# Modulation sums moved ahead, one block sum made by an accumulating DMA, FFN parts 8-6-8, other V banks, and queues ordered by the scheduler's other time line

## The chip, the cores and the metric

The kernel runs on one core of a Trainium2 chip. The metric is the device time of one execution in microseconds, the median over several runs. Before the change it is 997.38 us (three runs, 997.08 to 998.87).

## The reference

One decoder layer on 512 tokens of width 1024, batch 1, everything in float32: a half-step SwiGLU FFN (d_ff 2816), a token mixer, and a second half-step FFN. Each of the three is pre-RMSNorm with shift, scale and gate computed from a conditioning vector c:

```python
mod = silu(c) @ w_mod + b_mod
sh1, sc1, ga1, sh2, sc2, ga2, sh3, sc3, ga3 = split(mod, 9)
h = modulate(rms_norm(x, g_ffn1), sh1, sc1)
x = x + 0.5 * (1 + ga1) * ((silu(h @ w1_gate) * (h @ w1_up)) @ w1_down)
h = modulate(rms_norm(x, g_mix), sh2, sc2)
x = x + (1 + ga2) * hybrid_mixer(h, w_in, b_f, g_q, g_k, w_o)
h = modulate(rms_norm(x, g_ffn2), sh3, sc3)
x = x + 0.5 * (1 + ga3) * ((silu(h @ w2_gate) * (h @ w2_up)) @ w2_down)
```

The mixer projects h to q, k, v of 8 stick-breaking heads and 8 forgetting-attention heads of width 64 and to 8 forget gates, runs causal attention of both kinds, and projects the joined heads back.

## The kernel before, in words

**Numbers.** A float32 operand is split into `hi`, a copy rounded to the fast matmul type (ACT casts it), and `lo`, the rest (DVE subtracts). A product is three matmuls, hi by hi, hi by lo, lo by hi (`mm3`, L129 to L132). Tokens lie along the free axis: x and h are 8 tiles of 128 x 512 each, and h exists as `h["h"]` and `h["l"]`.

**Weights.** A weight tile of 128 x 1024 comes by a DMA on SP's queue into a `raw` buffer (4 of them), then ACT casts `hi` and DVE makes `lo` (4 buffers each). The chain raw, hi, lo runs some products ahead of TensorE as far as the buffers allow. ACT, DVE, POOL and SP each work off their queue in order, so an instruction that waits holds all that stand behind it.

**The FFN** (`ffn`, L508). The 22 tiles of d_ff are done in three parts, `FPARTS` (L21), of 8, 8 and 6. A part computes its gated tiles, `a[j]` as `ah` and `al` (`gated`, L406: ACT's Silu into `sg`, DVE's product `av`, ACT's cast `ah`, DVE's `al`), and then its down projection (`down`, L578): for each of the 8 output chunks e one weight tile, as many tiles by 3 matmuls as the part has (512 columns each), `update` of x[e] by DVE (L574). In most parts tiles come in pairs, `block_pair` (L442): the gate and up products of two tiles are done with a 2 x 2 block scheme that needs 7 products of 24 matmuls of 256 columns instead of 8. It loads four weight blocks r11, r12, r21, r22 into the four raw buffers and forms on DVE (`combined`, L459, into `bsum` buffers) s1 = r21 + r22, s2 = s1 - r11, s3 = r11 - r21, s4 = r12 - s2. The order of the products is r11, s2, s1, r12, s3, s4, r22. In the first FFN tiles 0 to 7 are done singly and 8 to 21 in 7 pairs; in the second tiles 4 to 21 in 9 pairs.

**The modulation.** mod has 9 x 8 chunks of 128 numbers. Two of the nine are needed at once; the other 56 chunks are filled into the first FFN (`mod_next`, L232): each is one 512 KB load on SP's queue into a `wm` buffer (4, shared with the `bsum` tiles) and one DVE multiply with a running sum (L216, `junk`). Before: 2 after each of tiles 4 to 7, 2 after each output chunk of a down projection (L598), 1 after each block pair (L529); of the 56, 47 are called for by the end of the last pair.

**The turn** (`turn`, L642). At the end of the first FFN and of the mixer, the last three output chunks are done in two halves of the tokens (H0, H1), each in a pass of as many steps as the part has tiles (mixer: 8). While the second pass runs, the norm of the first half is made: `mean` is asked for ahead of step 5 of that pass, ACT and DVE make the reciprocal root, and `make` the new h. The second half's norm follows inside the next stage, after its first matmuls (`finish`).

**The first V products** (L745 to L754). The mixer starts with two weight chunks by four token blocks, in two groups `sp` of four products each. A product takes one PSUM bank. Eight banks exist under four tags: mm 3, z 2, pt 2, o 1. Both groups take mm, z, mm, z. `v_out` copies a finished bank into V on DVE or ACT.

**What sets the order.** Each instruction is traced in program order; the framework's scheduler simulates the engines and lays out each engine's queue, earlier program order first among what is ready. Inside `manual_schedule` the program order itself is kept: for all engines in the first stage, for TensorE alone in the turns, the first V products and the mixer.

Of the kernel before, what the change touches and what calls it, by code (L numbers as in the profile page):

```python
# [12 lines left out]
ALU = mybir.AluOpType  # L13
# [4 lines left out]
D = 1024  # L18
KD = D // P
NF = 22  # L20
FPARTS = (8, 8, 6)  # L21
SPLIT1 = tuple(range(8, NF, 2))
SPLIT2 = tuple(range(4, NF, 2))
NPAIR = 4
# [11 lines left out]
def hybrid_layer(  # L36
# [18 lines left out]
    nc = tc.nc  # L55
# [176 lines left out]
    def mod_next(n):  # L232
        for _ in range(min(n, len(mod_queue))):
            m, d = mod_queue.pop(0)
            mod_chunk(m, d)
            if d < KD - 1:
                continue
            nc.vector.tensor_tensor(mod_col(m), mod_col(m), cols[:, m * KD : (m + 1) * KD], op=ALU.add)
            if m in (2, 8):
                nc.vector.tensor_scalar(g_col(m), mod_col(m), 1.0, 0.5, op0=ALU.add, op1=ALU.mult)  # L240
            elif m == 5:
                nc.vector.tensor_scalar(g_col(m), mod_col(m), 1.0, 1.0, op0=ALU.add, op1=ALU.mult)
            elif m == 4:
                g_norm(m, C_GM, 0, KD)
            elif m == 7:
                g_norm(m, C_G2, 0, KD)
# [193 lines left out]
        return out  # L440

    def block_pair(w, n_w, j, T, tmp):  # L442
        raws = []
        for n in range(4):
            raw = wpool.tile([P, 2 * S], F32, tag="raw", name=nm("raw"), bufs=4)
            nc.sync.dma_start(raw, w[n_w + n])
            raws.append(raw)
        r11, r12, r21, r22 = raws

        def parts(src):  # L450
            hi = wpool.tile([P, 2 * S], F32R, tag="hi", name=nm("hi"), bufs=4)
            lo = wpool.tile([P, 2 * S], F32R, tag="lo", name=nm("lo"), bufs=4)
            nc.scalar.copy(hi, src)  # L453
            nc.vector.tensor_tensor(lo, src, hi.bitcast(F32), op=ALU.subtract)  # L454
            return hi, lo

        def combined(x0, x1, op):
            t = block_tile(tmp)
            nc.vector.tensor_tensor(t, x0, x1, op=op)  # L459
            return t  # L460

        def whole_h(k0, sl):
            return [(h["h"][k0 + k][:, sl], h["l"][k0 + k][:, sl]) for k in range(KD // 2)]

        def summed_h(n):
            sl = slice(n * 256, (n + 1) * 256)
            return [(hi[:, sl], lo[:, sl]) for hi, lo in T]

        def product(b, wt, rhs, first, last):
            for u, sl in enumerate((H0, H1)):  # L470
                for k, (rh, rl) in enumerate(rhs):
                    lh, ll = wk(wt, 4 * u + k)
                    f, e = first and u == 0 and k == 0, last and k == KD // 2 - 1
                    nc.tensor.matmul(b[:, sl], lh, rh, start=f, stop=False, skip_group_check=True)  # L474
                    nc.tensor.matmul(b[:, sl], lh, rl, start=False, stop=False, skip_group_check=True)  # L475
                    nc.tensor.matmul(b[:, sl], ll, rh, start=False, stop=e, skip_group_check=True)  # L476

        def result(x0, x1, out=None):
            if out is None:
                out = tmp.tile([P, S], F32, tag="bres", name=nm("bres"), bufs=4)  # L480
            nc.vector.tensor_tensor(out, x0, x1, op=ALU.add)
            return out

        bx, by, bz = bank("o"), bank("mm"), bank("z")
        product(bx, parts(r11), whole_h(0, H0), True, True)
        p1 = tmp.tile([P, S], F32, tag="bres", name=nm("bres"), bufs=4)
        nc.scalar.copy(p1, bx)
        s1 = combined(r21, r22, ALU.add)
        s2 = combined(s1, r11, ALU.subtract)
        product(by, parts(s2), summed_h(1), True, True)  # L490
        q = result(by, p1)
        product(bz, parts(s1), summed_h(0), True, True)
        r = result(bz, p1)
        product(bx, parts(r12), whole_h(4, H0), False, True)
        s3 = combined(r11, r21, ALU.subtract)
        product(by, parts(s3), summed_h(2), False, True)
        c22 = result(by, r, r)
        s4 = combined(r12, s2, ALU.subtract)
        product(bz, parts(s4), whole_h(4, H1), False, True)
        c12 = result(bz, q, q)  # L500
        product(by, parts(r22), summed_h(3), False, True)
        c21 = result(by, p1, p1)
        return [
            gated(j, [(H0, bx[:, H0], bx[:, H1]), (H1, c12[:, H0], c12[:, H1])], tmp),
            gated(j + 1, [(H1, c22[:, H0], c22[:, H1]), (H0, c21[:, H0], c21[:, H1])], tmp),
        ]

    def ffn(first, w, wd, gm, startup, boundary, tmp, finish=None, split=()):  # L508
        pend = list(kb) if startup else []
        blocks = {}  # L510
        n_w = 0
        f0 = 0
        for part, nf in enumerate(FPARTS):
            last_part = part == len(FPARTS) - 1
            a = []
            halves_first = first and part == 0
            units = {}
            j = -1
            while j + 1 < nf:
                j += 1  # L520
                f = f0 + j
                if f in split:
                    if "T" not in blocks:
                        blocks["T"] = block_sums(tmp)
                    a += block_pair(w, n_w, j, blocks["T"], tmp)
                    n_w += 4
                    j += 1
                    if startup:
                        mod_next(1)  # L529
                    continue  # L530
                ps = []
                for u in range(2):
                    if pend:
                        ps.append(pend.pop(0))
                        continue
                    if halves_first and j < 2:
                        if j == 0 and u == 0:
                            ws, bs = [], []
                            for i in range(4):
                                ws.append(prep(w[n_w], D, nc.gpsimd if i == 3 else None))  # L540
                                n_w += 1
                                bs.append(bank("mm" if i % 2 == 0 else "z"))
                            late = [(i, k) for i in range(4) for k in range(KD // 2, KD)]
                            for sl in (H0, H1):
                                early = [(i, k) for k in range(KD // 2) for i in range(4)]
                                for i, k in early + (late if sl is H1 else sorted(late, key=lambda s: s[1])):
                                    lh, ll = wk(ws[i], k)
                                    mm3(bs[i][:, sl], lh, ll, h["h"][k][:, sl], h["l"][k][:, sl], k == 0, k == KD - 1)
                                    if sl is H0 and (i, k) == (3, 0):
                                        finish()  # L550
                            in_order.__exit__(None, None, None)
                            units = dict(enumerate(bs))
                        ps.append(units[2 * j + u])
                        continue
                    wt = prep(w[n_w], D)
                    n_w += 1
                    b = bank("z" if u else "mm")
                    for k in range(KD):
                        lh, ll = wk(wt, k)
                        mm3(b, lh, ll, h["h"][k], h["l"][k], k == 0, k == KD - 1)  # L560
                    ps.append(b)
                a.append(gated(j, [(FULL, ps[0], ps[1])], tmp))
                if startup and f > 3:
                    mod_next(2 if part == 0 else 3)
            if startup and part == 0:
                blocks["T"] = block_sums(tmp)
            if last_part and boundary != "end":
                in_order.__enter__()
            done = down(wd, a, f0, nf, gm, boundary if last_part else None, tmp)
            f0 += nf  # L570
        return done
# [172 lines left out]

    chunks = [v_weights(2), v_weights(3)]  # L745
    for sp in range(2):
        grp = [(ch, s, bank("mm" if s % 2 == 0 else "z")) for ch in chunks for s in (2 * sp, 2 * sp + 1)]
        for k in range(KD):
            for ch, s, b in grp:
                v_step(ch, s, k, b)  # L750
            if sp == 0 and k == 0:
                finish()
        for ch, s, b in grp:
            v_out(ch[0], s, b)  # L754
# [483 lines left out]
```

## Time and profile before

| | before |
|---|---|
| median of 3 runs | 997.38 us |
| the profiled execution, device time | 999.74 us |
| its span, first to last instruction | 998.0 us |
| mean granted TensorE clock | 0.993 |
| DVE, ACT, POOL busy | 773.7, 439.0, 119.0 us |
| HBM read | 125.92 MB |

The stages, in us from the span's start: norm and first weights to 23; the first eight products with modulation to 61; the rest of part 0 to 104.7 and its down projection to 148.2; four pairs to 229.0 and the down projection of part 1 to 273.6; three pairs to 334.0 and the down projection of part 2, with the turn, to 374.4; the mixer, with its turn, to 645; the second FFN to 994. A row of the table by stage has the stretch, its length, then for PE (matmul), PEld (weight load), DVE, ACT and POOL the busy time and in brackets the number of instructions that touch the stretch, then the granted TensorE clock (1.00 is full speed), the mean share of the 16 DMA engines, and GB/s. In a timeline or a list of groups, `out<-in` names tiles; a number in square brackets is idle time of the engine before the instruction, and what ended it. A row of waits names the waiting engine, tile and line, then who it waited for, and us in total, times, and the longest.

### The profile page before, as it was taken

To read this page: it belongs to the slowest core of one execution; us is meant where nothing else is said; L and a number is where in the kernel's file an instruction comes from. 1 tells how busy PE (TensorE), PEld (TensorE's weight loads), DVE (VectorE), ACT (ScalarE), POOL (GpSimd) and SP (SyncE) were. 2 spreads that over 40 slices of the span, in tenths; PEclk is the share of its full clock that TensorE was granted. 3 is DMA by queue.
4 is the path that set the end of the run, shared out by engine and by line. 5 is a ranking of instruction groups with operands and counts; after the bars stand their busy time and mean duration, and the time that the engine had idled before them with its cause. 6 is when DMAs were issued, how large, how long until landed. Compare 5 with 4: busy or idle time off the path is not lost.

```text
span 998.0 us, 15752 instructions
## 1 busy us (share of the span) xinstructions
PE 976.3 (98%) x6284; PEld 869.4 (87%) x6284; DVE 773.7 (78%) x1147; ACT 439.0 (44%) x686; POOL 119.0 (12%) x131
## 2 busy tenths in 40 slices
PE   8999999999999898999999999999999999999998
PEld 7888889998899798877887877998988999889997
DVE  7999967999879966688857687698855699556962
ACT  6344224443244425587556462364432444324430
POOL 1000000000000043065413335210000000000000
PEclk9999999999999899999999999999999999999999
DMA  9985933359634832411212111214252133521231
GB/s 358 316 277 154 343 135 106 121 159 309 235 104 122 260 107 65 127 55 53 64 54 73 44 43 65 85 37 133 76 147 93 55 116 103 150 85 64 96 117 63
DMA packets 37369, 129.04 MB, mean 129 GB/s; under 512 B 4400, under 2 KB 4656, under 8 KB 37296
## 3 DMA queue, kind: packets, MB, share of 16 engines
q1 hardware_dynamic: 35712, 125.88, 38.1%
q10 hardware_dynamic: 1584, 2.16, 0.6%
q8 instruction: 49, 0.80, 0.3%
q14 instruction: 24, 0.20, 0.1%
HBM read 125.92 MB, written 2.10 MB: 128 GB/s over the span
## 4 chain that ended last, share of the span: by engine, by line
PE 76%; DVE 14%; ACT 4%; DMA 3%; issue 2%; POOL 1%; SPq 0%; ACTq 0%; DVEq 0%; POOLq 0%
PE pt L131 8%; PE pt L132 8%; PE pt L130 8%; PE mm L130 5%; PE mm L132 4%; PE mm L131 4%; PE mm L476 3%; PE mm L475 3%; PE mm L474 3%; PE o L476 3%; PE o L475 3%; PE o L474 2%; PE z L476 2%; PE z L475 2%; PE z L474 2%; DVE lo L454 2%
## 5 line engine op out<-in xcount | busy, mean ns | idle before, releaser
L125 ACT CAST hi<-raw 128x1024 fp32r<-128x1024 f32 (+2 forms) x90 | 91.5, 1021 | 142.3 <-PE pt L131 61.3
L131 PE MATMUL pt<-al,hi 128*128 128x512 f32 (+1 forms) x334 | 131.1, 392 | 2.5 <-DVE al L415 2.5
L130 PE MATMUL pt<-ah,hi 128*128 128x512 f32 (+1 forms) x334 | 130.4, 391 | 0.6 <-ACT ah L414 0.6
L132 PE MATMUL pt<-ah,lo 128*128 128x512 f32 (+1 forms) x334 | 130.4, 390 | 0.0
L126 DVE TENSOR_TENSOR lo<-raw,hi 128x1024 fp32r<-128x1024 f32 (+2 forms) x89 | 108.0, 1216 | 28.8 <-ACT hi L125 28.3
L453 ACT CAST hi<-bsum 128x1024 fp32r<-128x1024 f32 x64 | 66.8, 1051 | 113.5 <-DVE bsum L459 61.3
L474 PE MATMUL mm<-th,hi 128*128 128x256 f32 x384 | 108.7, 283 | 0.0
L475 PE MATMUL mm<-tl,hi 128*128 128x256 f32 x384 | 108.7, 283 | 0.0
L476 PE MATMUL mm<-th,lo 128*128 128x256 f32 x384 | 108.7, 283 | 0.0
L574 DVE SCALAR_TENSOR_TENSOR x<-pt,gcol,x 128x512 f32<-128x512 f32 (+1 forms) x51 | 36.3, 712 | 67.2 <-PE pt L132 67.2
L454 DVE TENSOR_TENSOR lo<-bsum,hi 128x1024 fp32r<-128x1024 f32 x64 | 78.2, 1222 | 10.8 <-ACT hi L453 10.3
L453 ACT CAST hi<-raw 128x1024 fp32r<-128x1024 f32 x48 | 50.4, 1050 | 67.5 <-PE pt L131 30.5
L130 PE MATMUL mm<-hh,hi 128*128 128x512 f32 (+1 forms) x208 | 79.6, 383 | 0.0
L132 PE MATMUL mm<-hh,lo 128*128 128x512 f32 (+1 forms) x208 | 77.9, 374 | 0.6 <-DVE lo L126 0.6
L131 PEld LDWEIGHTS pt<-al,hi 128*128 128x128 f32 x334 | 63.4, 190 | 16.8 <-DVE al L415 4.0
L131 PE MATMUL mm<-hl,hi 128*128 128x512 f32 (+1 forms) x208 | 77.8, 374 | 0.2 <-DVE hl L170 0.2
L130 PEld LDWEIGHTS pt<-ah,hi 128*128 128x128 f32 x334 | 63.3, 190 | 14.4 <-ACT ah L414 1.4
L132 PEld LDWEIGHTS pt<-ah,lo 128*128 128x128 f32 x334 | 63.4, 190 | 12.9
L474 PEld LDWEIGHTS mm<-th,hi 128*128 128x128 f32 x384 | 73.7, 192 | 0.0
L475 PEld LDWEIGHTS mm<-tl,hi 128*128 128x128 f32 x384 | 73.7, 192 | 0.0
L476 PEld LDWEIGHTS mm<-th,lo 128*128 128x128 f32 x384 | 73.7, 192 | 0.0
L476 PE MATMUL o<-hh,lo 128*128 128x256 f32 x256 | 72.4, 283 | 0.0
(349 smaller groups left out, 2565.6 us busy)
## 6 DMA issues: line engine op xcount, KB each, us to landing
raw<-w SPq DMA_DIRECT2D x80, 512.0 KB, 3.6
wm<-wmod SPq DMA_DIRECT2D x72, 512.0 KB, 5.2
raw<-w1d SPq DMA_DIRECT2D x16, 512.0 KB, 6.3
raw<-wqk SPq DMA_DIRECT2D x16, 512.0 KB, 3.5
raw<-w2d SPq DMA_DIRECT2D x16, 512.0 KB, 4.2
raw<-w1s SPq DMA_DIRECT2D x8, 512.0 KB, 5.3
raw<-wo SPq DMA_DIRECT2D x8, 512.0 KB, 3.5
raw<-w1d SPq DMA_DIRECT2D x8, 384.0 KB, 5.9
```

The costliest lines, as they stand in the source:

```text
L125: nc.scalar.copy(hi, raw)
L126: (lo_engine or nc.vector).tensor_tensor(lo, raw, hi.bitcast(F32), op=ALU.subtract)
L130: nc.tensor.matmul(ps, lh, rh, start=first, stop=False)
L131: nc.tensor.matmul(ps, lh, rl, start=False, stop=False)
L132: nc.tensor.matmul(ps, ll, rh, start=False, stop=last)
L453: nc.scalar.copy(hi, src)
L454: nc.vector.tensor_tensor(lo, src, hi.bitcast(F32), op=ALU.subtract)
L474: nc.tensor.matmul(b[:, sl], lh, rh, start=f, stop=False, skip_group_check=True)
L475: nc.tensor.matmul(b[:, sl], lh, rl, start=False, stop=False, skip_group_check=True)
L476: nc.tensor.matmul(b[:, sl], ll, rh, start=False, stop=e, skip_group_check=True)
L574: nc.vector.scalar_tensor_tensor(out=x[e][:, sl], in0=ps[:, sl], scalar=g_col(gm)[:, e : e + 1], in1=x[e][:, sl], op0=ALU.mult, op1=ALU.add)
```

## The change

Six edits. (1) The parts of both FFNs are 8, 6, 8. (2) In `block_pair` s1 is no longer added by DVE: d21 is loaded into a raw buffer and d22 is added onto it by a second DMA that accumulates, issued from POOL's queue; the raw buffers then hold s1, r11, r12, r22. (3) s3 is formed as r22 - s2, which is the same r11 - r21. (4) Modulation: 3 chunks after each pair but the last, where there are none; the single tiles stay at 2. (5) The second group of the first V products takes banks pt, mm, pt, o. (6) The scheduler works against its other simulated time line (`schedule_with_timeline_sim`), which can change the order of every queue that isn't kept by hand.

```diff
-FPARTS = (8, 8, 6)
+FPARTS = (8, 6, 8)
...
     def block_pair(w, n_w, j, T, tmp):
-        raws = []
-        for n in range(4):
+        d11, d12, d21, d22 = (w[n_w + n] for n in range(4))
+
+        def load(src):
             raw = wpool.tile([P, 2 * S], F32, tag="raw", name=nm("raw"), bufs=4)
-            nc.sync.dma_start(raw, w[n_w + n])
-            raws.append(raw)
-        r11, r12, r21, r22 = raws
+            nc.sync.dma_start(raw, src)
+            return raw
+
+        s1 = load(d21)
+        nc.gpsimd.dma_start(s1, d22, accum_op=ALU.add)
+        r11, r12, r22 = load(d11), load(d12), load(d22)
...
-        s1 = combined(r21, r22, ALU.add)
         s2 = combined(s1, r11, ALU.subtract)
...
-        s3 = combined(r11, r21, ALU.subtract)
+        s3 = combined(r22, s2, ALU.subtract)
...
                     if startup:
-                        mod_next(1)
+                        mod_next(3 if f < NF - 2 else 0)
...
                 if startup and f > 3:
-                    mod_next(2 if part == 0 else 3)
+                    mod_next(2)
...
     for sp in range(2):
-        grp = [(ch, s, bank("mm" if s % 2 == 0 else "z")) for ch in chunks for s in (2 * sp, 2 * sp + 1)]
+        tags = iter(("pt", "mm", "pt", "o") if sp else ("mm", "z", "mm", "z"))
+        grp = [(ch, s, bank(next(tags))) for ch in chunks for s in (2 * sp, 2 * sp + 1)]
...
-    with tile.TileContext(nc) as tc:
+    with tile.TileContext(nc, schedule_with_timeline_sim=True) as tc:
```

## The prediction

> **What bounds the kernel now.** First the page: TensorE is busy for 976.3 of 998.0 us, so what isn't matmul time is 22 us at most, and the question is where it lies and whether the change reaches it.
>
> ```profile
> span 998.0 us, 15752 instructions
> PE 976.3 (98%) x6284; PEld 869.4 (87%) x6284; DVE 773.7 (78%) x1147; ACT 439.0 (44%) x686; POOL 119.0 (12%) x131
> ```
>
> Second, the view of waits, TensorE's alone: who it waited for, us in total, times, longest.
>
> ```profile
> PE mm L724 <- ACT hh L167: 2.8, 1, 2.8
> PE pt L131 <- DVE al L415: 2.5, 3, 1.1
> PE z L724 <- ACT V L713: 0.9, 1, 0.9
> PE pt L130 <- ACT ah L414: 0.6, 1, 0.6
> PE mm L131 <- DVE hl L170: 0.2, 1, 0.2
> ```
>
> Third, the table by stage, cut where TensorE's output tile changes (length, then busy us of PE, PEld, DVE, ACT, POOL, granted clock, DMA share, GB/s).
>
> ```profile
> 104.70:148.24 43.54, 43.54 (x193) 36.04 (x192) 35.00 (x50) 9.07 (x9) 0.00 (x0) 1.00 0.63 233
> 168.40:188.56 20.16, 20.16 (x171) 20.16 (x170) 19.32 (x26) 9.79 (x14) 0.00 (x0) 1.00 0.42 132
> 148.24:228.96 80.72, 80.72 (x674) 80.69 (x673) 71.79 (x89) 37.98 (x52) 0.00 (x0) 1.00 0.42 136
> 228.96:273.55 44.59, 44.00 (x194) 35.96 (x193) 39.20 (x58) 10.95 (x12) 0.00 (x0) 1.00 0.76 274
> 273.55:334.02 60.47, 60.47 (x505) 60.47 (x504) 53.83 (x70) 27.20 (x38) 0.00 (x0) 1.00 0.44 134
> 334.02:360.58 26.56, 23.99 (x92) 18.72 (x91) 20.65 (x31) 8.14 (x11) 10.66 (x7) 0.87 0.63 211
> 336.00:340.90 4.90, 2.39 (x9) 1.10 (x7) 4.90 (x10) 3.30 (x5) 0.00 (x0) 0.90 1.00 312
> 340.90:347.80 6.90, 6.84 (x18) 5.41 (x19) 6.73 (x10) 2.49 (x3) 1.61 (x1) 0.57 0.75 267
> 377.38:380.93 3.55, 3.55 (x14) 3.21 (x15) 3.55 (x10) 2.06 (x5) 0.00 (x0) 0.52 0.43 147
> 412.00:460.00 48.00, 43.95 (x218) 33.49 (x217) 39.73 (x66) 36.67 (x71) 24.20 (x26) 0.99 0.22 67
> 460.00:632.00 172.00, 169.09 (x1154) 138.61 (x1153) 122.28 (x198) 89.54 (x182) 63.85 (x68) 0.99 0.16 53
> 669.91:961.13 291.22, 290.59 (x1995) 271.46 (x1993) 212.97 (x249) 117.47 (x155) 0.00 (x0) 1.00 0.33 103
> 961.13:990.03 28.90, 28.90 (x129) 23.53 (x127) 11.25 (x15) 5.30 (x8) 0.00 (x0) 1.00 0.23 82
> ```
>
> These rows give TensorE's own pace. A down projection of 8 chunks by 8 tiles is 192 matmuls of 512 columns in 43.54 us: 0.2268 each. A block pair is 7 products of 24 matmuls, 168 of 256 columns in 20.16 us: 0.120 each. Held against it, the second FFN (669.91 to 961.13) loses nothing that could be won, and the loss sits in three places. (1) In the first FFN where block pairs give way to a down projection: 44.59 for 43.54 at 228.96, 1.05 lost; and at 334.02 26.56 us for 90 matmuls of 512 columns (5 chunks, 6 tiles, 3), which at full pace take 20.4: 6.1 lost, of it some 3 in waiting and 2.8 in the stretch behind, 18 matmuls in 6.9 us at a clock of 0.57. (2) At the turn to the mixer: the wait of 2.8 for the first h tile, then 3.55 us at a clock of 0.52 (1.7 lost), then 0.9 for a PSUM bank. (3) The mixer: 4.05 and 2.91 us not busy, many small waits.
>
> Why 334.02 is so bad shows in the timeline of ACT and DVE there:
>
> ```profile
> 333.99 0.83 ACT L125 CAST hi<-raw 128x768 fp32r<-128x768 f32 x1 [3.58 <-DMA raw<-w1d]
> 336.68 1.28 ACT L98 ACT_TABLE_LOAD   x1
> 336.12 1.22 DVE L216 SCALAR_TENSOR_TENSOR junk<-wm,c_bc 128x1024 f32<-128x1024 f32 x1
> 337.27 0.69 DVE L415 TENSOR_TENSOR al<-av,ah 128x512 fp32r<-128x512 f32 x1
> ```
>
> ACT stands 3.58 us on a cast of a down weight that lands late, with the last Silu queued behind it; DVE puts a modulation sum (L216) ahead of the al that TensorE waits for. Both are the modulation's doing: its loads stand before the down weights in SP's queue, its sums fill DVE.
>
> **The change part by part.** Sums go against the profiled execution, 999.74 us (998.0 span, 1.7 around it); the median of the runs is 997.38, 2.4 lower, and I take the same difference off that.
>
> *Parts 8, 6, 8.* The number of matmuls stays. Over the last part of each FFN the chunks that are cut into halves (3 at the first, 1 at the end) get 2 more tiles each: (3+1) x 2 x 3 = 24 matmuls of 512 columns become 48 of 256, 24 x (0.240 - 0.2268) = +0.3 us. In exchange each pass of the turn has 8 steps for 6. The mean of the first half is asked for at step 5 of the second pass; from there 13 steps of 3 x 0.12 are left now, 4.7 us, and 19 afterwards, 6.8: 2.1 us more cover over the wait of 2.8. The trace holds the same function with 8 steps per pass at the mixer's end, where the wait is 0.2 (L131 on hl). I take that: -2.6. The half clock that follows only this turn goes with it: -1.7.
>
> The last pairs-to-down transition now has 8 tiles, so the last al is due at the 22nd matmul, 4.8 us in, not at the 16th. It has no modulation left (next item) and resembles those of the second FFN, which lose nothing. The table load of 1.28 is still there; I leave 0.5 for it: -6.1 + 0.5.
>
> The middle transition gets 6 tiles, with modulation around it. Today with 8 tiles it loses 1.05; the last al is now due two tiles, 6 x 0.2268 = 1.4 us, earlier: 2.4 us lost, +1.4. Bounds: 0.3, the row 961.13 (28.90 for 126 matmuls, 28.58 at full pace: 6 tiles without modulation), and 6.1, the row 334.02 (6 tiles with it, and with a half clock behind). It is nearer to 1.05, since the table load isn't there: I take 2.4.
>
> *Modulation: 3 sums per pair instead of 1, none at the last.* The 56 sums stay; by the code 9 of them come behind the last pair today and none afterwards. From 148.24 to 334 DVE has 25:
>
> ```profile
> L216 DVE SCALAR_TENSOR_TENSOR junk<-wm,c_bc 128x1024 f32<-128x1024 f32 x25 | 30.5, 1220 | 2.9 <-DMA wm<-wmod 2.8
> L459 DVE TENSOR_TENSOR bsum<-raw,raw 128x1024 f32<-128x1024 f32 x12 | 14.7, 1222 | 3.5 <-DMA raw<-w 3.3
> raw<-w SPq DMA_DIRECT2D x80, 512.0 KB, 3.6
> wm<-wmod SPq DMA_DIRECT2D x72, 512.0 KB, 5.2
> raw<-w1d SPq DMA_DIRECT2D x8, 384.0 KB, 5.9
> GB/s 358 316 277 154 343 135 106 121 159 309 235 104 122 260 107 65 127 55 53 64 54 73 44 43 65 85 37 133 76 147 93 55 116 103 150 85 64 96 117 63
> ```
>
> Afterwards up to 9 more fall there, 9 x 1.3 = +12 us of DVE; the additions of s1 go, 7 x 1.2 = -8.5. From 148.24 to 334.02 DVE is busy 71.79 + 39.20 + 53.83 = 164.8 of 185.8 us, 89%; afterwards some 168 less 2 (shorter down weights) of 175 (the middle down is 48 x 0.2268 = 10.9 us shorter), 95%. On average it fits. The middle down is where it doesn't: per chunk TensorE needs 18 x 0.2268 = 4.1 us, in which two modulation tiles and one weight tile, 1.44 MB, want 353 GB/s; the best slice has 358, the stretch with all queues full 312. At 312 the 8 chunks' 11.5 MB take 36.9 us for 32.7: 4 us behind, covered by what SP loads ahead, or not. Bounds 0 and +4; nearer to the covered side, since at 274 GB/s the DMAs are at a share of 0.76: +1. What is queued behind: on SP the next down weight, for which ACT's cast, then all of ACT, waits.
>
> *s1 added by the DMA.* One DVE addition per pair goes, 16 in all. In the second FFN nothing waits for it, so nothing is won there; in the first its gain is in the 95% above. New is an accumulating load on POOL's queue that waits for d21. Behind it on POOL nothing stands in pair stages (POOL 0.00 in all their rows). With it and two more modulation tiles a pair loads 1.6 MB more, 132 GB/s becoming some 210, which collides with nothing. How long the accumulate takes, no row shows. Its room is read from one pair, which starts at 208.72:
>
> ```profile
> 204.77 1.22 DVE L459 TENSOR_TENSOR bsum<-raw,raw 128x1024 f32<-128x1024 f32 x1 [0.92 <-DMA raw<-w]
> 206.24 1.22 DVE L459 TENSOR_TENSOR bsum<-bsum,raw 128x1024 f32<-128x1024 f32 x1
> 212.12 1.22 DVE L454 TENSOR_TENSOR lo<-bsum,hi 128x1024 fp32r<-128x1024 f32 x1
> ```
>
> s1's last reader (lo, 212.12) ends 4.6 us into the pair, then the buffer may be loaded for the next; s2 is formed 2.5 us before the next pair (206.24 before 208.72). 20.16 - 4.6 - 2.5 = 13 us, less 3.6 for the plain load: 9.4 us for the accumulate. The nearest rows: 3.6 for a plain load, and 11.8 for twice the 5.9 of one under load, since it reads two sources. I take some 6 to 7, hidden: 0.
>
> The Trainium skill, "DMA: Bandwidth & Descriptors", section on SWDGE, HWDGE and iDMA, says that accumulation is only for transfers whose descriptors GpSimd writes into SBUF rings, and its section on the anatomy of one DMA fits them with 2.0 us plus the bytes by 436 GB/s, an estimate of 3.2 us here, which would leave the sum as it is. "GPSIMD Engine Reference", Key points, speaks against the change: GpSimd contends for SBUF with DVE instructions of two SBUF inputs, which are most of what DVE does in a pair. No run here shows either yet.
>
> *Other banks for the first V products.* The second group takes pt, the third mm, pt and o, all idle since the turn; the wait for the evacuation of a z bank goes: -0.9. Next late is nothing: the scores' first banks come later.
>
> *Other time line.* It reorders queues, not work. In the second FFN, with DVE at 213 of 291 us, there is room for any sane order. In the mixer the order decides; bounded by its own idle time, -7, and by all its 220 us waiting like the worst stretch, 4.05 of 48: 18.6, less the 7 that are there, +11.6. Nothing in the trace favours a side: 0.
>
> Sum: +0.3 - 2.6 - 1.7 - 5.6 + 1.4 + 1 - 0.9 = -8.1 us, 989.3.
>
> **The rivals.** *The loss moves to the middle transition and stays as large.* For it: the same tile count and the same modulation flood as at 334.02 today, more of it per pair. Against: no table load, and 1.05 today. Then 6.1 instead of 2.4 and 4 instead of 1: -8.1 + 3.7 + 3 = -1.4, 996.0, no change.
>
> *The mixer's queues get worse.* For it: nothing else in the change touches it, and its norm chains cross four engines. Against: today's order has no claim to be good. Priced above: -8.1 + 11.6 = +3.5, 1000.9, slower. It decides against the change from some 10 us of new waits in 412 to 632.
>
> *The accumulate lands too late* in every pair: each us over 9.4 costs 16. At 11.8 it is +38 - 8 = +30, 1027; the change is lost from 9.9 on.
>
> *The half clock isn't owed to these waits.* At 334 the longest is 1.1 us and they sum to some 3; then 2.8 and 1.7 stay lost: -8.1 + 4.5 = -3.6, 993.8, still faster. The Trainium skill, "TensorE: Matmul & The Clock Gate", section on HAM oscillation, has the clock halved by idle gaps over some 3.4 us; by that rule no wait here (1.1 and 2.8 at most) would do it. The trace disagrees so far: both halvings follow right behind waits.
>
> **How the numbers follow.** Forecast 989.3 (the likeliest case's own range 983 to 995.3): 0.59. Half clock stays: 0.05. Loss moved: 0.13. Mixer worse: 0.15. Accumulate late: 0.08. A measurement of this kernel can tell about 0.2%, 2 us. Faster 0.64, same 0.13, slower 0.23. The low end is the sum with the residues (0.5, 1.4, 1) gone and 3 of the mixer's 7 won: 983. The high end takes in the mixer's case with some us beyond: 1003; the accumulate's case and tails are left out.
>
> **What would show it.** Right: the wait L724 on hh at 0.2 or so and no clock under 0.9 between 300 and 400 us; no L216 after the last pair; the last down at 0.2268 per matmul; the wait of L724 on V gone; the middle down some 35 us long. Wrong: a middle down of 38 us or more with waits on al or ah and a half clock behind (loss moved); waits at s2's casts in every pair of both FFNs (accumulate); the mixer longer by several us.

## The result, and the profile after

The change makes the kernel slower: 1029.02 us median (4 runs, 1026.73 to 1031.45) beside 998.12 for the kernel before, run beside it, ratio 1.0321 with a 95% interval of 1.0301 to 1.0342. The forecast was 989.3 with a range up to 1003.0. The profiled execution took 1026.73 us, its span is 1025.0, the mean granted clock 0.987 (0.993 before).

From the page of the kernel after, the span, the engines' busy times, and two rows of POOL's accumulating load (the group of its issues, then the row of issues with the median time to landing):

```profile
span 1025.0 us, 15857 instructions
PE 985.1 (96%) x6308; PEld 874.9 (85%) x6308; DVE 753.2 (73%) x1131; ACT 440.6 (43%) x686; POOL 130.2 (13%) x147
L451 POOL DMA_DIRECT2D raw<-w x16 | 14.0, 878 | 520.5 <-DMA raw<-w 165.9
raw<-w POOLq DMA_DIRECT2D x16, 512.0 KB, 5.5
```

DVE has 20 us less to do, as the dropped additions say, and yet TensorE's time without matmul grows from 22 to 40 us. Its busy time grows by 8.8 us with 24 matmuls more, which at full clock would be 0.3: the rest is matmuls at a lower clock. So what was lost is waits and what follows waits. For the table by stage the runs are cut at the same places of the program. The last down reaches to the second step of the first V products (behind the matmul of the second half's mean); what is called the mixer reaches from there to the second pass of its turn; what is called its turn is that pass and the four single tiles of the second FFN; what is called the second FFN starts with its first block pair. After first (three pairs, the middle down, four pairs, last down, mixer, its turn, second FFN), then before (mixer, its turn, second FFN):

```profile
147.74:208.82 61.08, 60.68 (x505) 60.51 (x504) 55.37 (x76) 28.73 (x39) 0.86 (x1) 1.00 0.63 205
208.82:249.91 41.09, 35.70 (x146) 27.86 (x145) 36.34 (x58) 8.92 (x12) 1.72 (x2) 0.96 0.85 263
249.91:332.76 82.85, 80.85 (x673) 80.67 (x672) 71.62 (x93) 39.56 (x53) 1.72 (x2) 1.00 0.51 160
332.76:384.59 51.83, 50.02 (x286) 43.65 (x285) 24.89 (x39) 17.59 (x27) 11.25 (x9) 0.97 0.30 93
384.59:653.20 268.61, 251.55 (x1616) 207.21 (x1615) 185.10 (x326) 144.67 (x285) 95.94 (x108) 0.97 0.18 56
653.20:714.52 61.32, 57.03 (x368) 52.43 (x367) 51.53 (x86) 31.20 (x50) 6.68 (x5) 0.97 0.39 102
714.52:1021.60 307.08, 304.40 (x2065) 282.54 (x2063) 194.93 (x233) 113.13 (x148) 6.08 (x7) 0.99 0.38 110
```

```profile
381.32:636.08 254.76, 246.82 (x1616) 204.14 (x1615) 182.71 (x322) 144.91 (x283) 96.01 (x108) 0.99 0.18 59
636.08:692.62 56.54, 55.72 (x369) 50.85 (x368) 52.06 (x88) 30.14 (x49) 5.03 (x3) 1.00 0.32 103
692.62:994.50 301.88, 301.88 (x2059) 281.29 (x2057) 205.26 (x241) 112.25 (x148) 0.00 (x0) 1.00 0.31 98
```

Up to the mixer the kernel after is 3.3 us later (384.59 for 381.32), where the forecast had it some 8 earlier; the mixer takes 13.9 us more, its turn 4.8, the second FFN 5.2. Those 27 us are the difference of the two spans. The mixer, a stage in which the change replaces no instruction, is half of it. Of what the mixer loses, 9.1 us are idle (17.1 for 7.9 without matmul), the other 4.7 are TensorE's busy time, 251.55 for 246.82, at a clock of 0.97 for 0.99.

TensorE's waits in the kernel after (us in total, times, longest) name many small ones on three engines. Those that the forecast wanted gone are gone: between 375 and 400 us, where the first turn ends and the first V products are made, the view shows no wait of TensorE. The longest of the list:

```profile
PE pt L1016 <- POOL beta L1010: 5.2, 4, 1.5
PE pt L130 <- DVE x L577: 4.2, 3, 2.3
PE z L957 <- ACT fw L105: 3.4, 3, 1.4
PE mm L131 <- DVE hl L170: 3.0, 1, 3.0
PE pt L1016 <- POOL fw L999: 2.5, 3, 2.0
PE mm L478 <- DVE bres L485: 2.4, 2, 2.0
PE pt L130 <- ACT ah L414: 2.3, 2, 1.4
```

### The profile page after: what moved, and what is told of

It reads as the page before. It is cut to its first block, busy times and chain, and to the rows that moved or that the text cites. A ratio compares the mean times of both kernels' runs of the same rounds, so it can differ in the third digit from the quotient of the medians.

```text
span 1025.0 us, 15857 instructions
## 1 busy us (share of the span) xinstructions
PE 985.1 (96%) x6308; PEld 874.9 (85%) x6308; DVE 753.2 (73%) x1131; ACT 440.6 (43%) x686; POOL 130.2 (13%) x147
## 4 chain that ended last, share of the span: by engine, by line
PE 75%; DVE 11%; DMA 6%; issue 3%; ACT 3%; POOL 1%; SPq 0%; DVEq 0%; POOLq 0%; ACTq 0%
PE pt L130 5%; PE mm L130 5%; PE pt L131 5%; PE pt L132 5%; PE mm L131 5%; PE mm L132 5%; DMA raw<-w 4%; PE mm L478 4%; PE mm L479 4%; PE mm L480 4%; PE o L480 3%; PE o L479 3%; PE o L478 3%; PE z L480 3%; PE z L479 3%
## 5 line engine op out<-in xcount | busy, mean ns | idle before, releaser
L130 PE MATMUL pt<-ah,hi 128*128 128x512 f32 (+1 forms) x328 | 128.9, 395 | 7.6 <-DVE x L577 4.2
L131 PE MATMUL pt<-al,hi 128*128 128x512 f32 (+1 forms) x328 | 129.0, 395 | 2.3 <-DVE al L415 2.3
L132 PE MATMUL pt<-ah,lo 128*128 128x512 f32 (+1 forms) x328 | 128.0, 392 | 0.0
L457 ACT CAST hi<-raw 128x1024 fp32r<-128x1024 f32 x64 | 67.3, 1052 | 121.6 <-PE pt L131 48.8
L458 DVE TENSOR_TENSOR lo<-raw,hi 128x1024 fp32r<-128x1024 f32 x64 | 77.6, 1219 | 8.7 <-ACT hi L457 8.6
L130 PEld LDWEIGHTS pt<-ah,hi 128*128 128x128 f32 x328 | 62.7, 191 | 23.3 <-ACT hi L457 3.4
L130 PE MATMUL mm<-hh,hi 128*128 128x512 f32 (+1 forms) x208 | 81.0, 389 | 1.3 <-ACT hh L167 1.3
L457 ACT CAST hi<-bsum 128x1024 fp32r<-128x1024 f32 x48 | 50.5, 1052 | 69.2 <-PE mm L479 27.0
L451 POOL DMA_DIRECT2D raw<-w x16 | 14.0, 878 | 520.5 <-DMA raw<-w 165.9
L216 DVE SCALAR_TENSOR_TENSOR junk<-wm,c_bc 128x1024 f32<-128x1024 f32 x56 | 68.4, 1221 | 9.9 <-DMA wm<-wmod 9.6
```

The source lines that it names most:

```text
L130: nc.tensor.matmul(ps, lh, rh, start=first, stop=False)
L131: nc.tensor.matmul(ps, lh, rl, start=False, stop=False)
L132: nc.tensor.matmul(ps, ll, rh, start=False, stop=last)
L216: nc.vector.scalar_tensor_tensor(out=junk, in0=wm, scalar=1.0, in1=c_bc, op0=ALU.mult, op1=ALU.mult, accum_out=mods[:, i : i + 1])
```

## The experiments

The ratio is to the kernel before, run beside it on the same chip, with its 95% interval.

### The time line, and the accumulated s1

`e1_old_line` is the kernel after without the other time line; `e2_line_only` is the kernel before with it:

```diff
-    with tile.TileContext(nc, schedule_with_timeline_sim=True) as tc:    # e1, from after
+    with tile.TileContext(nc) as tc:
-    with tile.TileContext(nc) as tc:                                     # e2, from before
+    with tile.TileContext(nc, schedule_with_timeline_sim=True) as tc:
```

`e3_plain_new_line` is the kernel after with s1 added by DVE from four plain loads, as before; `e4_plain_old_line` is that without the other time line:

```diff
-        s1 = load(d21)
-        nc.gpsimd.dma_start(s1, d22, accum_op=ALU.add)
-        r11, r12, r22 = load(d11), load(d12), load(d22)
+        r11, r12, r21, r22 = load(d11), load(d12), load(d21), load(d22)
...
+        s1 = combined(r21, r22, ALU.add)
...
-        s3 = combined(r22, s2, ALU.subtract)
+        s3 = combined(r11, r21, ALU.subtract)
```

> The changed kernel with the scheduler's usual time line, all other edits kept. Theory Q (the queue order laid out by the other time line costs the time: it puts block sums that wait for the accumulate ahead of updates of x, and spoils the mixer's order): the 27 us of the mixer (13.8), of the mixer's turn (4.8), of the second FFN (5.4) and of the first FFN (3.3) go, and what the forecast counted for the other edits is seen: 987 to 993. Rival A (the accumulating DMA costs the time in any order, because its landing, 4.3 to 9.4 us, comes on top of the plain load): the two FFNs stay slow, only the mixer's 14 us come back: 1010 to 1016. Rival M (the middle down projection with 6 tiles and two modulation chunks per output chunk is bound by its loads in any order): that stage stays at 41.1 us for 32.7; the whole 995 to 999.

> The kernel before with nothing changed but the scheduler's other time line. Theory Q: slower than before by 15 us or more, 1013 to 1030, with the mixer at some 268 us from the first V product to its turn (before 254.8). Rival A: as before to 4 us slower where the mixer is concerned; the second FFN at 301 us, since nothing accumulates. If the mixer is no longer than before here, the V banks, not the time line, lengthen it.

> The changed kernel, other time line kept, but s1 formed by DVE from four plain loads as before, in the old way of forming s3 too. Theory Q in its narrow form (the harm in the FFNs is the accumulate's wait put early in DVE's queue by this time line): the second FFN falls from 307.1 to 301.7 us, the middle down stage loses a few us less, the mixer stays at 268: 1015 to 1021. Theory Q in its wide form (any order of this time line is bad): the second FFN stays at 305 or more. Rival A: 1010 to 1016, and the same kernel with the usual time line no better than the kernel before.

> The changed kernel with the usual time line and s1 formed by DVE: parts 8, 6, 8, modulation moved ahead, V banks alone. Theory Q: 989 to 995, the accumulate adding little to it either way. Rival A: some 10 us faster than the accumulating kernel with the usual time line. Rival M: 996 to 1000, the middle down stage at 38 us or more with a half clock behind its waits.

| | median us | ratio | 95% |
|---|---|---|---|
| e1_old_line | 1002.37 | 1.0064 | 1.0047 to 1.0080 |
| e2_line_only | 1026.34 | 1.0311 | 1.0285 to 1.0337 |
| e3_plain_new_line | 1024.40 | 1.0286 | 1.0268 to 1.0305 |
| e4_plain_old_line | 1001.59 | 1.0053 | 1.0034 to 1.0071 |

The other time line alone costs as much as the whole change. But taking it out does not bring the forecast's gain: e1 and e4 are half a per cent slower than before. So there are two losses. The accumulate is neither: without it the kernel is 0.1% faster under the usual time line (e4 beside e1) and 0.35% under the other one (e3 beside the kernel after), and both pairs of intervals overlap. It has a small part under the other time line all the same: the second FFN takes 303.2 us in e3, 307.1 with the accumulate. The stages of e2, mixer, its turn and second FFN, show the first loss without any other edit:

```profile
390.55:655.89 265.34, 249.36 (x1617) 206.44 (x1615) 182.56 (x320) 143.43 (x281) 96.43 (x108) 0.98 0.18 56
655.89:718.20 62.31, 58.02 (x368) 53.47 (x367) 52.77 (x87) 31.24 (x50) 4.90 (x3) 0.95 0.30 94
718.20:1021.20 303.00, 302.59 (x2059) 281.23 (x2057) 204.12 (x241) 112.86 (x148) 0.00 (x0) 1.00 0.31 97
```

The first FFN and its turn, up to the mixer, take 9.2 us more (390.55 for 381.32), the mixer 10.6, the mixer's turn 5.8, the second FFN 1.1.

### Is it the order, and whose

The time line could change something besides the order. So each of these kernels, all from before, is traced twice: the first trace, with the usual time line, gives each engine's queue; in the second, with the other, consecutive instructions of the engines named are tied by dependencies that only order them. Only the list of engines differs:

```diff
+    for names in (queues or {}).values():          # the usual order of the engines that are held
+        chain = [traced[n] for n in names if n in traced]
+        for a, b in zip(chain, chain[1:]):
+            tc.add_manual_dep(b, a.name, ORDER_ONLY, reason="kept order")
```

f_dve holds DVE; f_but_dve ACT, POOL, SP and TensorE; f_act ACT; f_pe_sp TensorE and SP; f_all all five; f_dve_act DVE and ACT.

> The kernel before under the other time line, which alone made it 3.1% slower, but DVE's queue held in the order of before; ACT, POOL, SP and, outside its hand-kept stretches, TensorE are laid out by the other time line around it. Theory D (DVE's queue carries the harm: it is laid out breadth first, all ht of a turn ahead of all hl, weight splits ahead of the scans and al that TensorE waits for): nearly all of the 30 us come back, 996 to 1004, the mixer's turn with a wait of 0.2 for hl instead of 3.0. Theory C (ACT's queue carries it, casts of weights not due ahead of Silu and of scores): still 1015 or more. Theory L (loads and TensorE's own order): still 1010 or more.

> The counterpart: ACT, POOL, SP and TensorE held in the order of before, DVE's queue alone laid out by the other time line. Theory D: 1015 or more. Theory C or L: 996 to 1004. If both this and its counterpart stay near before, the harm needs both queues changed at once; if both are slow, each queue harms by itself.

> As the first of these, but ACT's queue held in the order of before and the rest free. Theory C: 996 to 1006. Theory D: 1015 or more, the scheduler laying out DVE as breadth first as without it.

> TensorE's and SP's queues held in the order of before, DVE, ACT and POOL free. Theory L: 996 to 1006. Theories D and C: 1018 or more, as with nothing held.

> The kernel before under the other time line with all five queues held in the order of before. Theory Q (the order of the queues is all that the time line changes): as before within 0.3%, 995 to 1002. Rival B (the time line also changes which buffer an instruction gets and so what it waits for): slower by 5 us or more.

> As with DVE's queue alone held, which left it 2.6% slower, but DVE's and ACT's together. Theory P (the harm is in how DVE's and ACT's queues interleave; each link of hi to lo, of Silu to al, of score to weight crosses between the two, so one held and the other free clash): most of it comes back, 997 to 1006. Rival (loads and TensorE's own order, free here, carry a part of their own): 1010 or more, with the second FFN still slow.

| held in the usual order | median us | ratio | 95% |
|---|---|---|---|
| all five | 996.95 | 1.0003 | 0.9991 to 1.0014 |
| DVE and ACT | 999.21 | 1.0029 | 1.0017 to 1.0041 |
| all but DVE | 1021.54 | 1.0226 | 1.0210 to 1.0241 |
| TensorE and SP | 1021.78 | 1.0230 | 1.0208 to 1.0252 |
| DVE | 1025.46 | 1.0256 | 1.0227 to 1.0285 |
| ACT | 1027.50 | 1.0282 | 1.0266 to 1.0298 |

With all queues held nothing is left of the loss: it is order alone. DVE's new order by itself, with every other queue as before, costs 2.3%. That DVE held alone would bring back most was expected and is wrong: either of DVE and ACT held alone leaves 2.6 to 2.8%, both together leave 0.3%. A `hi` on ACT and its `lo` on DVE, an `hh` and its `hl`, alternate, so one queue in the old order would wait for the other in the new one; this is argued from the code, and no run tells these links apart. The orders of TensorE and SP have a smaller part: holding them takes the loss from 3.1 to 2.3%, and holding ACT and POOL besides takes off nothing more. With DVE and ACT held, the mixer and its turn have nearly the times of before:

```profile
374.92:631.53 256.61, 247.66 (x1617) 204.46 (x1615) 182.74 (x324) 144.06 (x285) 95.50 (x108) 0.99 0.19 58
631.53:688.54 57.01, 56.26 (x368) 51.00 (x367) 52.92 (x88) 31.04 (x51) 5.03 (x3) 1.00 0.32 102
```

### One order by itself

What the new order does is seen best at the mixer's turn. DVE's timeline of e2 there:

```profile
665.51 0.88 DVE L161 SCALAR_TENSOR_TENSOR ht<-x,gcol,hold 128x256 f32<-128x256 f32 x2
666.31 0.42 DVE L656 TENSOR_TENSOR hold<-hold,sqh 128x256 f32<-128x256 f32 x1
666.65 2.46 DVE L161 SCALAR_TENSOR_TENSOR ht<-x,gcol,hold 128x256 f32<-128x256 f32 x6
669.02 0.48 DVE L574 SCALAR_TENSOR_TENSOR x<-pt,gcol,x 128x256 f32<-128x256 f32 x1
669.42 3.25 DVE L170 SCALAR_TENSOR_TENSOR hl<-ht,mods,hh 128x256 fp32r<-128x256 f32 x8
```

All eight `ht` come ahead of the first `hl`, though TensorE needs `hl` of tile 0 first; before, they alternate:

```profile
644.10 0.86 DVE L161 SCALAR_TENSOR_TENSOR ht<-x,gcol,hold 128x256 f32<-128x256 f32 x2
644.89 0.41 DVE L656 TENSOR_TENSOR hold<-hold,sqh 128x256 f32<-128x256 f32 x1
645.22 0.87 DVE L170 SCALAR_TENSOR_TENSOR hl<-ht,mods,hh 128x256 fp32r<-128x256 f32 x2
```

`b_breadth` puts this one order into the kernel before; `n_depth` puts the alternation into e2, at this turn alone:

```diff
+    for _, b in made:                                   # b_breadth, from before: made = [(ht, hl), ...]
+        tc.add_manual_dep(b, made[7][0].name, order, reason="breadth")
...
+    for a, b in zip(made, made[2:]):                    # n_depth, from e2_line_only
+        tc.add_manual_dep(b[0], a[1].name, order, reason="depth")
```

> The kernel before with the usual time line, and one order forced at the mixer's turn alone: all eight ht of the first half on DVE ahead of its first hl, as the other time line has it; nothing else is held. Theory (breadth ahead of depth is what the turn loses under the other line): TensorE's first matmul on hl waits 2 to 3 us for 0.2 and a half clock may follow, 2 to 5 us in all, 999 to 1002, ratio 1.002 to 1.005. Rival (the turn's loss under the other line, 62.3 for 56.5 us, comes from what it does to the update, the squares and the mean ahead of ht): no change, ratio 0.999 to 1.001.

> The kernel before with the other time line, and at the mixer's turn alone ht and hl of the first half held in alternation (an ht not before the hl two back). Theory: the wait of 3.0 us on hl goes, the turn comes back by 2 to 5 us, ratio some 1.026 to 1.029 for 1.031, and the rest of the 30 us stays where it is, in the first FFN and the mixer, since there is no one place. Rival: the turn's length stays at 62 us.

b_breadth: 998.69 us, ratio 1.0019 (1.0006 to 1.0032); n_depth: 1026.01 us, 1.0291 (1.0270 to 1.0312), an interval that overlaps e2's. The profiles say more than the totals. In b_breadth TensorE waits 3.0 us for `hl` as in e2, and the turn takes 58.3 us for 56.5; in n_depth that wait is 0.6 and the turn takes 57.4 for e2's 62.3:

```profile
636.12:694.37 58.25, 55.29 (x368) 51.11 (x367) 52.25 (x88) 30.32 (x49) 5.04 (x3) 1.00 0.31 100
```

```profile
658.11:715.46 57.35, 55.45 (x369) 51.09 (x367) 52.63 (x87) 31.35 (x50) 4.74 (x3) 1.00 0.33 102
```

So this order alone costs 1.7 us here and taking it out of the new line gives back 5.0 at the turn: in e2 a wait of 1.3 on `hh` stands right ahead of the one on `hl`, and a half clock follows (last section); in n_depth the 1.3 is still there, the half clock is not. Not all of the 5.0 reaches the total, since n_depth's mixer ahead of the turn takes 268.3 us for e2's 265.3. It is one of many places: with it mended the kernel is still 2.9% slower.

### The second loss: the modulation

`g_parts` is e4 with the modulation as before, one sum after each pair; `h1_spread` has one after each pair but the last and spreads the others by hand over the downs; `g_mods` is the kernel before with the modulation's edit alone; `g_acc` is g_parts with the accumulated s1.

```diff
-                        mod_next(3 if f < NF - 2 else 0)     # g_parts and g_acc, from e4 and e1
+                        mod_next(1)
...
-                        mod_next(1)                          # h1_spread, from g_parts
+                        mod_next(1 if f < NF - 2 else 0)
-            mod_next(2)
+            mod_next({0: 2 + e % 2, 8: 1, 14: 3 if e else 2}[f0])
...
-                        mod_next(1)                          # g_mods, from before
+                        mod_next(3 if f < NF - 2 else 0)
```

> Parts 8, 6, 8 and the V banks alone, with the usual time line, s1 on DVE and the modulation as before (1 per pair, 2 per output chunk). Theory F (the middle down of 6 tiles asks for its loads faster than they come, and starves the pair behind it): that pair still starts late, the middle down and the pairs behind it lose 6 us or more, in all 994 to 1000. Rival (3 modulation sums per pair overload DVE): with 1 per pair again the pairs lose nothing, 986 to 991.

> Parts 8, 6, 8 and V banks, usual time line, s1 on DVE, and the 56 modulation chunks spread by room: 2 or 3 per output chunk in the first down, 1 per pair, 1 per chunk in the middle down, 14 in the last. Theory F: the middle down's loads fall from 353 to some 225 GB/s, the pair behind it starts on time, and the gains that were forecast stay (final transition 5, turn 4, bank 0.9): 987 to 992. Rival (last down: the sums there again stand ahead of al and cost a half clock): 994 to 998.

> The kernel before with the modulation's edit alone: 3 sums after a pair, none after the last, parts still 8, 8, 6, plain s1, usual time line. Theory A (the loss arises in a middle down of 6 tiles: its 2 modulation tiles and one weight tile per 4.1 us keep the next pair's blocks back): with 8 tiles there is 1.3 us more per chunk, 1.44 MB in 5.4 us is 267 GB/s, the pairs behind lose 3 us at most, and the last down without modulation gains up to 5.6: 992 to 997, ratio 0.994 to 0.999. Theory B (3 sums per pair overload DVE whatever the down): pairs behind the middle down still lose 8 to 11, the gain at the last down stays: 1000 to 1004, ratio 1.002 to 1.006.

> Parts 8, 6, 8, the V banks and the accumulated s1 (from POOL's queue), with the modulation at one sum per pair as before and the usual time line: all edits but the time line and the 3 sums. Theory (the accumulate lands inside its 9.4 us and frees DVE of 1.2 us per pair which nothing waits for): as without it, ratio 0.993 to 0.997. Rival (landings of up to 9.4 us make s2 late in some pairs): 4 us or more slower than without it, ratio 0.998 or above.

| | median us | ratio | 95% |
|---|---|---|---|
| g_parts | 990.57 | 0.9949 | 0.9934 to 0.9963 |
| g_acc | 991.31 | 0.9948 | 0.9931 to 0.9964 |
| h1_spread | 992.70 | 0.9961 | 0.9947 to 0.9976 |
| g_mods | 1000.17 | 1.0027 | 1.0015 to 1.0039 |

g_parts differs from e4 in the one argument and is 1% faster (0.9949 for 1.0053): some 10 us for 3 sums per pair instead of 1. With the accumulate the same one argument, e1 beside g_acc, costs some 12 (1.0064 for 0.9948). Parts and banks by themselves win half a per cent, g_parts and g_acc are the fastest kernels of this study, and spreading the sums further wins nothing. The first FFN by stage, of e4 (middle down, four pairs, last down) and of g_parts (the same three):

```profile
208.31:242.54 34.23, 33.37 (x146) 26.74 (x145) 31.82 (x54) 8.35 (x11) 0.00 (x0) 1.00 0.92 320
242.54:334.50 91.96, 84.98 (x674) 83.96 (x674) 83.94 (x104) 40.65 (x56) 0.00 (x0) 0.96 0.45 149
334.50:382.56 48.06, 47.83 (x286) 42.49 (x285) 25.96 (x39) 17.29 (x27) 11.20 (x9) 1.00 0.34 101
```

```profile
209.25:243.86 34.61, 33.52 (x146) 26.87 (x145) 32.24 (x53) 8.48 (x12) 0.00 (x0) 1.00 0.78 280
243.86:324.69 80.83, 80.83 (x674) 80.69 (x673) 76.52 (x98) 39.07 (x54) 0.00 (x0) 1.00 0.50 157
324.69:373.09 48.40, 47.79 (x286) 42.48 (x285) 37.63 (x57) 18.72 (x29) 13.82 (x9) 1.00 0.53 175
```

In e4 the four pairs behind the middle down take 92.0 us for the 80.6 that their matmuls need; in g_parts 80.8. The middle down itself takes no more in e4 than in g_parts. g_mods was to tell whether the six-tile middle down's loads do it (A) or the sums on DVE (B). Its time is B's, but the place is neither's. Its stages are the first four pairs, a stretch out of them, the middle down (8 tiles here), the three pairs behind it, the last down:

```profile
147.67:234.18 86.51, 82.77 (x674) 82.28 (x672) 79.43 (x106) 39.88 (x54) 0.00 (x0) 0.98 0.48 162
196.00:208.00 12.00, 12.00 (x102) 12.00 (x101) 12.00 (x20) 5.33 (x7) 0.00 (x0) 1.00 0.72 262
234.18:277.73 43.55, 43.55 (x195) 36.05 (x194) 40.27 (x58) 9.57 (x11) 0.00 (x0) 1.00 0.80 285
277.73:338.20 60.47, 60.47 (x506) 60.47 (x504) 53.53 (x69) 29.02 (x40) 0.00 (x0) 1.00 0.39 125
338.20:381.12 42.92, 39.28 (x221) 34.39 (x219) 26.19 (x44) 16.03 (x28) 10.93 (x9) 0.94 0.35 106
```

The loss, 5.8 us, lies in the pairs ahead of the middle down, right after a stretch in which DVE is busy for 12.00 of 12 us; behind the middle down nothing is lost. So A falls: the short down isn't needed. DVE's sum per pair fits it: the prediction's row 148.24 has 71.79 us of DVE in four pairs, 17.9 each with one sum; two more at 1.22 make 20.4 for a pair of 20.16. DVE falls behind within a few pairs. A rival is that the added modulation loads, on SP's queue too, keep the block loads back. The waits speak against it: from 190 us to the end of g_mods' first four pairs DVE waits 0.2 us for a block load and ACT 1.8, while ACT waits 8.5 for DVE's block sums; in e4's four pairs DVE waits 0.7 for a block load. Where DVE's lead runs out differs, behind the middle down in e4, ahead of it in g_mods; why there was read from no run. With the accumulate a pair is 1.22 lighter, 19.2, yet e1 is no faster than e4: its middle down loses 6.0 us and its pairs 5.8. DVE's waits of e1 between 200 and 340 us show late loads there:

```profile
DVE bsum L463 <- DMA raw<-w: 6.7, 3, 6.0
```

The one of 6.0 is s2's, near the end of the middle down, for the accumulated s1. From the start of the middle down, s1's plain load goes out after 13.9 us and the accumulate after 20.9, landing 8.8 later; in g_acc, with one sum per pair, they go out after 7.6 and 13.4, and TensorE loses 1.0 in that stage. So in e1 the loads were late from the start, as it seems behind the larger number of modulation loads and sums, and the accumulate, which can only go out behind a plain load, added its own landing. How much of the 11.8 us each of the two costs wasn't taken apart.

## Why the prediction was wrong, point by point

**The step that failed: "Other time line ... Nothing in the trace favours a side: 0".** By itself it is +30 us (e2), more than all other terms together. Three things in that step were wrong. It was bounded in the mixer alone, with "room for any sane order" in the second FFN and nothing said of the first FFN and the turns: 16 of e2's 27 us by stage lie outside the mixer, 9.2 in the first FFN with its turn, 5.8 in the mixer's turn and 1.1 in the second FFN. For the second FFN the room held as long as the loads were plain. It is not room in a queue, though: in the kernel after, DVE is busy for 195 of 307 us there and still stood here, with the update of x that TensorE's bank waited for queued behind a block sum that waited for an accumulating load:

```profile
873.00 0.96 DVE L126 TENSOR_TENSOR lo<-raw,hi 128x768 fp32r<-128x768 f32 x1
880.69 1.23 DVE L463 TENSOR_TENSOR bsum<-raw,raw 128x1024 f32<-128x1024 f32 x1 [6.73 <-DMA raw<-w]
881.83 0.75 DVE L577 SCALAR_TENSOR_TENSOR x<-pt,gcol,x 128x512 f32<-128x512 f32 x1
```

That is the 2.3 us wait of L130 on x in the list above, and 3.4 us at a clock of 0.51 follow it at 882.8. Second, the upper bound (+11.6) took the worst stretch of the existing order as the worst that an order can do; the mixer alone lost 13.9. In e2's mixer DVE ran three `lo` for weights of the turn in one go, the first of them not used by TensorE before 630.3 and the last not before 651.5, ahead of the scan that POOL's `beta` and then TensorE stood waiting for (before, two scans stand between the first of the three and the others):

```profile
618.39 3.50 DVE L126 TENSOR_TENSOR bw<-raw,bw 128x1024 fp32r<-128x1024 f32 x3 [0.87 <-PE z L953]
621.81 0.55 DVE L1016 TENSOR_TENSOR PT<-pt,keep_sb 128x384 f32<-128x384 f32 x1
622.28 0.94 DVE L1003 TENSOR_TENSOR_SCAN R<-keep,free_sb 128x383 f32<-128x383 f32 x1
```

Third, "favours no side" was itself a choice. The kernel before lost 22 us of 998 to everything but matmuls and some 7 more to three stretches at half clock (13.6 us in all), so an order drawn anew had at most 29 to win and no such limit on the other side. That this order is broad where the old one is deep is read from the traces and was tried at one place; which places make up the rest stays open.

**The rival that came nearest**, the mixer's queues getting worse, had the mechanism and the sign, at 0.15, and priced one stage of four.

**Modulation, +1 with bounds 0 and +4.** It is +10 without the accumulate (e4 beside g_parts) and +12 with it (e1 beside g_acc). The step weighed DVE over 148 to 334 us, pairs and downs together, and found 95%, counting the additions of s1 that go as relief. The count itself was right: in e1 DVE is busy for 164.0 us from the first pair to the last down, against 173.8 of matmuls at full pace there, 94%. What failed is the step from that room to a cost of 1: e1 loses 11.8 us there all the same, with DVE standing for a late accumulating load. Without the relief, in e4, the room is gone, per pair (over 100%) and over the stretch (171.8 of 173.8, 99%). The second check, plain loads in the middle down, wasn't the limit: with the flood of e4 that down took 34.2 us for 32.7.

**Parts and banks.** Here the sum held by stage. From the first pair to the mixer g_parts takes 224.3 us (148.78 to 373.09) and the kernel before 233.1: -8.8, where the forecast's terms for this stretch, without the modulation's +1 and the bank's -0.9, which falls behind it, make -8.2. The wait on `hh` at the turn, its half clock and the bank's wait are gone; the last down is 48.4 for a forecast of 48.6 (47.3 before, 10.9 for two tiles more, less 9.6); the middle down loses 1.9 for 2.4. The forecast gave two reasons for the last transition, eight tiles and no modulation left, and either goes most of the way: by the code g_parts still has nine sums there, and e4, with none, is only 0.3 faster in that stage; g_mods, with six tiles and none left, takes 42.9 for 47.3 before, though the wait of 2.8 on `hh` stays. In medians g_parts wins 5 to 6 us, less than by the profiled executions; that of the kernel before lies 2.4 above its median.

**The accumulate at 0**: right by itself (g_acc beside g_parts). The median landing of 5.5 us is inside the 9.4 of room. The plain fit given from the Trainium skill, "DMA: Bandwidth & Descriptors", section on the anatomy of one DMA, 3.2 us, is too low for it here, though not by enough to matter. The sign given for its rival, waits at s2's casts in every pair, is absent from the kernel after; in the second FFN what the late loads did is the one 2.3 us wait above with the half clock behind it, 3.9 us beside e3. With the flood they cost more (e1, above). The contention that the Trainium skill, "GPSIMD Engine Reference", Key points, speaks of can't be seen: DVE's two-input sums take 1.22 us with and without it.

**The loss moved to the middle transition.** Its sign did come in the kernel after, a middle down of 41.1 us (8.4 lost) with waits on `ah` and `al` and a half clock behind them. It takes the other time line or the accumulate beside the flood: e4, with the flood alone, loses 1.6 there, e3, with the other time line, 4.4, e1, with the accumulate, 6.0.

**The half clock owed to waits**: right at the turn. With the wait gone the clock of g_parts is 1.00 in all its rows above.

## What to carry to other kernels

An edit that lays out queues anew is not an edit with a cost near zero: a kernel whose bounding engine loses 2% has little to win from it and much to lose, and after this case I would forecast it slower unless the profile shows waits that the new order removes. Room for added work is counted engine by engine, over the stretch and per period of the loop that must absorb it, and a share of 95% is no proof that it fits: an engine that works in order loses its lead where it stands for a late load. And changes that come as one should be taken apart first: here a gain of half a per cent lay under two losses.

## What the runs showed of the hardware

TensorE's clock halved in these runs behind waits of 3.3 us and less. In e2's turn waits of 1.3 and 3.0 us follow each other from 665 on, TensorE is idle for 3.3 of 4 us, and then the clock is halved for 6.8:

```profile
665.00:669.00 4.00, 0.66 (x4) 0.26 (x2) 3.96 (x10) 2.75 (x7) 0.20 (x1) 0.99 0.60 196
669.00:675.80 6.80, 5.85 (x23) 5.50 (x24) 3.67 (x10) 2.28 (x7) 0.00 (x0) 0.51 0.00 0
```

In b_breadth the same wait of 3.0 us, with none close ahead of it, leaves the clock at 1.00 (its row above); there the wait is the whole cost. Neither length nor closeness decides by itself: in the kernel after a wait of 2.0 us at 497.8, in the mixer, with only one of 0.25 close ahead, is followed by 3.4 us of half clock, one of 2.0 at 267.3, in a pair stage with no other wait near, by none. Between 60 us and the last matmul that kernel has seven such stretches of 3.4 or 6.8 us, the one before three, g_parts one. The Trainium skill, "TensorE: Matmul & The Clock Gate", section on HAM oscillation, gives the rule as no idle gaps over some 3.4 us; the trace disagrees with it as a bound on single gaps. The section on the clock gate itself has activity watched in free-running windows of 3.4 us: the lengths seen here, 3.4 and 6.8, agree. Why the same wait halves the clock in one place and not in another stays open, since no run here shows the windows themselves. For this kernel a wait of 2 to 3 us costs its own length and, where the clock halves behind it, 1.7 or 3.4 us more (half of the stretch).
